# A two-level Strassen MLP: another order of the pair's steps, two splits of w2 in other buffers, two sums of x two steps later

## The chip, the cores and the metric

The kernel runs on one core of one Trainium2 chip. The metric is the device time of one execution in microseconds (us), the median of the runs. A core has five engines with instruction queues of their own: TensorE (PE, matmuls), VectorE (DVE), ScalarE (ACT), GpSimd (POOL) and SyncE (SP, which here only issues DMAs). An engine takes its instructions in the order in which the program gives them, and waits at one until its operands and its buffer are free.

## The reference

```python
h = x @ w1                                             # x (8, 1024, 1024), w1 (1024, 4096)
h = 0.5 * h * (1 + tanh(sqrt(2 / pi) * (h + 0.044715 * h ** 3)))
return h @ w2                                          # w2 (4096, 1024)
```

Input and output are float32. The kernel multiplies 16-bit floats and sums in float32.

## The kernel before

The 8192 rows of x are worked off in eight superblocks of 1024 tokens (0 to 7). For each, the first multiplication makes h = x·w1, ScalarE applies the gelu and leaves g in SBUF in 16 bits, and the second multiplication makes g·w2. Both use Strassen's scheme, seven products of halves in place of eight: an operand of a product is a quarter block of the matrix (11, 12, 21, 22) or a sum of such blocks, made on DVE or POOL in 16 bits, and the result needs float32 additions of what the products left in PSUM. Superblocks 0 and 1 use one level. From superblock 2 on ("late") a second level is used inside products 1 to 7, in both multiplications. What the second level of w1 and w2 needs (inner sums) is made once, in superblocks 0 and 1, and stored in DRAM; that of x has to be made for each superblock.

**The late first multiplication** (`matmul1_late`, L780-822). The columns of h are worked off in eight pairs of chunks, j = 0 to 7, and a ninth round, j = 8, finishes the last one. What a pair does is the list `PAIR` (L30-36), 108 steps, walked once for each j. A step that has a ' behind its name belongs to the pair before. So the list is a software pipeline written out, and each engine's order is the order of its steps in the list (the instructions are pinned in program order). The first letter names the kind:

- `m` and `h` are PE's: `m36` is inner product 6 of product 3 (two matmuls of 256 columns into a quarter of a PSUM bank), `h40` half of product 4, which has one level (four matmuls of 512 columns). In pair 0 products 1, 5 and 7 are whole too: they have no inner sums to wait for.
- `z`, `e`, `s`, `u` are float32 sums on DVE that read PSUM (L138); `a`, `c`, `p`, `q` and `z11`, `z51`, `z71` are copies on ScalarE (L165); `g` is a gelu on ScalarE (L510).
- `v` is a float32 sum on POOL (L764), `d` a difference of two blocks of g (L516; on POOL, for pair 0 on DVE).
- `x35` is inner sum 5 of the x operand of product 3, made on DVE; `X35` is the same on POOL (both L355, `inner_sum`). They are made once in a superblock: those without a mark while j = 0, those with a ' while j = 1. The sums of product 7 lie in a tile "xi", the others in tiles "gc". Sum 6 reads sum 7 or 5, and sum 4 or 3 reads sum 6, of the same product.
- `k` is one of four sums of w1 for the next pair, on POOL (L315, tiles "mu"), from pair 2 on. `b` and `r` are sums of blocks of g that the second multiplication begins with, on POOL (L1059).

At j = 8 the table `BEGIN` starts the first quarters of the second multiplication behind the named steps. At the end of each round j = 0 to 3 `x_cast_paced` (L475-480) brings a quarter of the next superblock's x into DRAM in 16 bits: POOL copies two elements of a chunk of g as a mark, which makes it wait for that chunk, and then issues two casting DMAs (L472). For j > 3 SP's transposing DMAs read them. The weights of a pair (`StoredHalf`, loads at L284) are loaded by SP up to three pairs ahead into tiles of the pool `up`.

**The late second multiplication** (`matmul2`, class `Inner`): seven products of seven steps each in the order 4, 1, 2, 5, 6, 7, 3. The table `FILL_2` names the jobs that DVE does behind step n of product m, as "mn: jobs". `n6` and `n3` are sums 6 and 3 of the next superblock's x blocks (two of the operands of its first multiplication); they stand at 33 and 34, steps 3 and 4 of the last product.

**Superblock 1's second multiplication** (`matmul2_made`) has one level. Beside it, the table `FILL` (second half of the kernel's two tables, one for superblock 0 and one for 1) makes the inner sums of w2, "splits": `p34` is inner sum 4 of w2's operand of product 3 (`split_jobs`, L968-982). One split is two DVE sums of 128x1024 into a tile of 4 KB for each partition, and a DMA issued by POOL (L980) that stores it.

**Buffers.** The pool `up` has 24 tiles of 4 KB named "u", for nearly everything that passes; `mp` two of the same size named "mu", for the made sums of w1; `gcp` four "gc"; `xip` one "xi"; `tp` nine float32 tiles "tmp"; PSUM has eight banks. A tile is handed out in turn, and its first writer waits until the last user of the buffer is done, be it an engine or a storing DMA.

The marking copy and the split's allocation are these lines:

```python
done = g["22"][:, 2 * j - 1, :] if j else now.temps["a", 0]          # L813, matmul1_late
nxt["xb"] = x_cast_paced(sb + 1, done, 2 * j, nxt.get("xb"), True)
t[n] = unit(NI // 2, OH // 2)                                        # L977, split_jobs: a "u" tile
```

Of the kernel before, what the change touches and what calls it, by code (L numbers as in the profile page):

```python
# [9 lines left out]
DT = mybir.dt.float16  # L10
# [4 lines left out]
P = 128  # L15
# [12 lines left out]
MADE_HALF = 3  # L28
ROOM = (("11", 4), ("11", 8), ("11", 12), ("22", 4), ("22", 8), ("22", 12), ("21", 4), ("21", 8), ("21", 12))
PAIR = """  # L30
X37' s1' g220' m11 g110' m15 u1' m36' m27' c1 e30' r1' X35 x55 m51 z11 z32' h41' m16 k7 z23'
m32' m33' z24' z51 g221' x54' v0' k6 x15 m56 m55 z12 x36 m37' q1' g120' e31' x75 m71 X34' c5 m52
z71 m24' m13 g111' z52 m12 m17 z33' m76 m75 z34' z13 m53 m57 v1' m21 m25 b a0 x17 h60 m34' z53
c7 r0 p0 m14 x77 k5 g210' z72 k3 e20 m77 s0 g211' m54 z73 m73 X74' z21 m72 x57 a1 X56 h40 x16
g121' m26 d' u0 z22 m31 p1 z31 x76 q0 e21 r2' h61 m74 m23 m22 m35 X14
""".split()
BEGIN = {"m32": (0,), "m33": (1,), "m24": (2, 3), "m34": (4,)}
SPLIT_IN_M1 = ()


def slots(table):
# [24 lines left out]
    ;51:g311 g312;52:g321 g322;53:a67;54:a66;55:a65;56:a63  # L66
    ;61:n5;63:a77;64:a76;65:a75;66:a73;67:n7
    ;71:y11 y12;72:y21 y22;73:a37;74:a36 w11;75:a35 w12;76:a33 w21;77:w22
    ;31:z11 z12;32:z21 z22;33:n6;34:n3""".replace("\n    ", ""))


@with_exitstack
def kernel(
# [18 lines left out]
    NI = I // P // 2  # L92
    OH = O // 2
# [10 lines left out]
    mp = ctx.enter_context(tc.tile_pool(name="mp", bufs=2))  # L104
# [29 lines left out]
    def unit(rows, cols):  # L134
        return up.tile([P, rows, cols], DT, name="u")

    def tt(out, in0, in1, op, pin=False):
        i = nc.vector.tensor_tensor(out=out, in0=in0, in1=in1, op=op)  # L138
        if pin:
            tc.keep_in_program_order(i)  # L140
# [12 lines left out]
    def chunks(t):  # L153
        return t.rearrange("p o (c n) -> p o c n", c=QC)
# [203 lines left out]
    def x_blocks():  # L358
        return {b: unit(KH, HT) for b in ("22", "21", "12", "11")}
# [107 lines left out]
    def x_cast(s, after, rows=range(0, SB, P), xb=None):  # L467
        if xb is None:
            xb = xdram.tile([SB, H], DT, name="xb")
        with tc.issue_after(after.ins):  # L470
            for q in rows:
                nc.gpsimd.dma_start(out=xb[q:q + P, :], in_=x2[s * SB + q:s * SB + q + P, :])  # L472
        return xb

    def x_cast_paced(s, g_chunk, q, xb, pin=False):  # L475

        mark = nc.gpsimd.tensor_copy(out=pace, in_=g_chunk[:, :2])
        if pin:
            tc.keep_in_program_order(mark)
        return x_cast(s, mark, range(q * P, (q + 2) * P, P), xb)  # L480

    def x_transpose(xb, dma, blocks=None, which=range(4)):
        blocks = blocks or x_blocks()
        for b, t in [list(blocks.items())[i] for i in which]:
            a, k = int(b[0]) - 1, int(b[1]) - 1
            for j in range(KH):
                dma(
                    t[:, j, :],
                    xb[a * HT:(a + 1) * HT, (k * KH + j) * P:(k * KH + j + 1) * P],
                    transpose=True,  # L490
                )
        return blocks
# [30 lines left out]
    def g_tiles():  # L523
        return {b: g_tile(b) for b in ("11", "12", "21", "22")}
# [249 lines left out]
    def matmul1_late(xs, sb, quads, g):  # L774
        n = NI // 2
        nxt = {}
        early = Inner(4, g["22"])
        made = set(xs.inner)
        last = None
        for j in range(n + 1):  # L780
            if j < n:
                quads += [StoredHalf(i) for i in range(len(quads), min(j + 3, n))]
                now = Pair(j, quads[j], xs, g)
            for key in PAIR:
                late = key.count("'")
                key = key.rstrip("'")
                if key[0] in "xX":
                    if late == j and int(key[1]) not in made:
                        xs.inner_sum(int(key[1]), int(key[2]), nc.vector if key[0] == "x" else nc.gpsimd)
                elif key == "b":  # L790
                    if 4 <= j < n:
                        early.make_quarter(7, j - 4)
                elif key[0] == "r":
                    if j == n - 1 + late:
                        early.make_quarter(6, int(key[1]))
                elif key[0] == "k":
                    if MADE_HALF <= j + 1 < n:
                        quads[j + 1].make(int(key[1]))
                elif late:
                    for i in BEGIN.get(key, ()) if j == n else ():  # L800
                        early.begin(i)
                    if last is not None:
                        last.run(key)
                elif j < n:
                    now.run(key)
            last = now
            if j == n:
                break
            if j == n - 1:
                early.load(STEPS[:3])  # L810
            if sb < NSB - 1:
                if j < 4:
                    done = g["22"][:, 2 * j - 1, :] if j else now.temps["a", 0]  # L813
                    nxt["xb"] = x_cast_paced(sb + 1, done, 2 * j, nxt.get("xb"), True)
                if j == 3:
                    nxt["blocks"] = x_blocks()
                if j > 3:
                    x_transpose(nxt["xb"], load_in_order, nxt["blocks"], range(j - 4, j - 3))
        blocks = nxt.get("blocks")
        return g, early, None if blocks is None else XOps(blocks)  # L820
# [145 lines left out]
    def split_jobs(m, pieces):  # L966
        t = {}

        def operand(v, h):
            if isinstance(v, int):  # L970
                return t[v][:, h * QC:(h + 1) * QC, :]
            k, b = int(v[0]) - 1, int(v[1]) - 1
            return chunks(pieces()[2 * k + h])[:, b]

        def make(n):
            u, op, v = W_SUM[n]
            t[n] = unit(NI // 2, OH // 2)  # L977
            for h in range(2):
                tt(t[n][:, h * QC:(h + 1) * QC, :], operand(u, h), operand(v, h), op, True)
            nc.gpsimd.dma_start(out=in_d[m][:, SUMS.index(n)], in_=t[n])  # L980

        return [lambda n=n: make(n) for n in SUMS]
# [242 lines left out]
    for sb in range(NSB):  # L1225
        if sb < 2:
            g, nxt = matmul1(xs, sb, quads, first if sb == 0 else None)
            xs, quads = matmul2_made(sb, g, None if sb else quads[-1].keep_raw, nxt)
            continue
        g, early, nxt = matmul1_late(xs, sb, quads, g_late or g_tiles())  # L1230
        g_late, quads = matmul2(sb, g, early, nxt)
        xs = nxt
# [30 lines left out]
```

## Time and profile before

| | |
|---|---|
| median of 3 runs | 1485.46 us (1484.85 to 1492.23) |
| profiled execution | 1482.05 us |
| its span, first to last instruction | 1480.3 us |
| mean granted clock of TensorE | 0.996 |
| busy: PE / DVE / ACT / POOL | 1455.5 / 1223.9 / 690.4 / 622.0 us |
| matmuls | 10635 |
| moved by DMA | 472.72 MB, mean 319 GB/s |

The profile is a trace of one execution. PE, DVE, ACT and POOL are the engines above; SPq is the queue of SyncE, DMA issues only. A group or an instruction is named by its line in the kernel, its engine and operation, and out<-in by the program's tile names; "[2.86 <-DVE ps L138]" says that the engine had been idle for 2.86 us and that an instruction of DVE, of line 138, ended that wait. The list of waits sums these up by engine: total us, times, longest. The chain of waits follows the work that ended last back from the end of the span and is shown in order of time: start, us, who held it. A line of windows gives for a stretch of time its length, the busy time of PE, PE's weight load (PEld), DVE, ACT and POOL with the number of their instructions, PE's granted clock as a share of full speed, the share of the DMA engines' time in use, and GB/s.

### The profile page before, as it was taken

The page shows a single profiled execution, that of the slowest core. Times are in us where ns is not written, and L with a number is a line of the kernel's source. Part 1 is how long each engine was busy: PE and PEld are TensorE (multiplying, and loading weights), DVE is VectorE, ACT ScalarE, POOL GpSimd, SP SyncE. Part 2 cuts the span into 40 slices and gives each one's busy share as a digit, 9 for nine tenths or more (in the row PEclk, how much of TensorE's full clock was granted, in tenths as well). Part 3 has the DMA queues.
Part 4 walks back from the last instruction along what each step waited for, and adds up shares of the span by engine and source line. Part 5 has one row for each costly group of instructions (what it writes and reads, how often), then busy time and mean ns, then how long its engine had stood idle before and what let it go on. Part 6 is the DMA issues. An engine that isn't in the chain of part 4 may idle for free.

```text
span 1480.3 us, 28812 instructions
## 1 busy us (share of the span) xinstructions
PE 1455.5 (98%) x10635; PEld 1038.9 (70%) x10635; DVE 1223.9 (83%) x2031; ACT 690.4 (47%) x1406; POOL 622.0 (42%) x632
## 2 busy tenths in 40 slices
PE   8999999999999999999999999999999999999998
PEld 5444444444467887678877788677886778877887
DVE  5656668657788999889998899888998889988897
ACT  5665116631078511784128831388213872168610
POOL 1541232212369312782047811487104971158411
PEclk9999999999999999999999999999999999999999
DMA  9999999879999999999999999999999999997897
GB/s 328 345 346 382 280 362 343 293 253 264 346 325 232 328 335 381 361 234 367 312 377 347 227 376 316 360 320 239 375 334 358 292 282 343 368 383 233 294 299 233
DMA packets 205709, 472.72 MB, mean 319 GB/s; under 512 B 75648, under 2 KB 80768, under 8 KB 204672
## 3 DMA queue, kind: packets, MB, share of 16 engines
q1 hardware_dynamic: 177632, 373.35, 73.4%
q0 software_dynamic: 27936, 97.53, 22.0%
q8 instruction: 83, 1.36, 0.4%
q14 instruction: 58, 0.48, 0.1%
HBM read 370.15 MB, written 115.34 MB: 328 GB/s over the span
## 4 chain that ended last, share of the span: by engine, by line
PE 68%; DVE 3%; issue 1%; DVEq 0%
PE ps L1082 35%; PE ps L712 22%; PE ps L497 11%; DVE tmp L138 1%; DVE gc L355 1%; DVE ps L138 1%; DVE xi L355 0%; DVE u L138 0%; DVEq L138 0%
## 5 line engine op out<-in xcount | busy, mean ns | idle before, releaser
L165 ACT COPY tmp<-ps 128x512 f32<-128x512 f32 (+1 forms) x536 | 280.6, 536 | 294.9 <-PE ps L1124 139.2
L497 PE MATMUL ps<-u 128*128 128x512 f16 x1552 | 363.9, 379 | 0.0
L1082 PE MATMUL ps<-u,gc 128*128 128x256 f16 x2688 | 300.3, 273 | 0.0
L1082 PEld LDWEIGHTS <-gc 128*128 128x128 f16 x2688 | 263.0, 98 | 30.5
L138 DVE TENSOR_TENSOR tmp<-tmp,ps 128x256 f32<-128x256 f32 (+1 forms) x372 | 198.4, 544 | 79.4 <-PE ps L1124 29.5
L497 PEld LDWEIGHTS <-u 128*128 128x128 f16 x1552 | 152.1, 98 | 146.8 <-issue 0.5
L138 DVE TENSOR_TENSOR u<-u 128x1024 f16<-128x1024 f16 (+3 forms) x292 | 221.2, 800 | 36.2 <-DMA w_d<-u 20.9
L839 POOL DMA_DIRECT2D out_dram<-u x70 | 63.8, 952 | 442.3 <-DVE u L138 239.5
L1082 PE MATMUL ps<-u,g 128*128 128x256 f16 x2016 | 231.8, 273 | 0.0
L712 PEld LDWEIGHTS <-u 128*128 128x128 f16 x2026 | 197.7, 98 | 48.1 <-issue 0.8
L165 ACT COPY u<-ps 128x512 f32<-128x512 f32 (+1 forms) x134 | 78.0, 587 | 327.9 <-PE ps L1082 320.9
L1082 PEld LDWEIGHTS <-g 128*128 128x128 f16 x2016 | 197.3, 98 | 24.1
L712 PE MATMUL ps<-u 128*128 128x256 f16 x1342 | 204.9, 273 | 0.3 <-DVE tmp L138 0.2
L138 DVE TENSOR_TENSOR ps<-tmp,ps 128x256 f32<-128x256 f32 x444 | 177.3, 424 | 25.5 <-PE ps L712 16.0
L510 ACT ACTIVATE g<-tmp 128x512 f16<-128x512 f32 x282 | 173.4, 634 | 47.0 <-DVE tmp L138 46.7
L1124 PE MATMUL ps<-u,g 128*128 128x512 f16 x768 | 168.3, 382 | 2.8 <-DVE tmp L138 2.8
L138 DVE TENSOR_TENSOR u<-u,ps 128x512 f32<-128x512 f32 x216 | 146.4, 682 | 26.4 <-PE ps L1082 17.7
L510 ACT ACTIVATE g<-ps 128x512 f16<-128x512 f32 x230 | 137.7, 599 | 51.8 <-PE ps L712 42.8
L1124 PEld LDWEIGHTS <-g 128*128 128x128 f16 x768 | 75.5, 98 | 94.9 <-issue 5.3
L764 POOL TENSOR_TENSOR tmp<-tmp 128x512 f32<-128x512 f32 x96 | 121.8, 1269 | 41.8 <-ACT tmp L165 37.8
L138 DVE TENSOR_TENSOR tmp<-ps,tmp 128x512 f32<-128x512 f32 x126 | 87.0, 690 | 55.9 <-PE ps L497 45.9
L138 DVE TENSOR_TENSOR gc<-g,gc 128x2048 f16<-128x2048 f16 x78 | 95.0, 1218 | 0.6
(68 smaller groups left out, 1470.4 us busy)
## 6 DMA issues: line engine op xcount, KB each, us to landing
u<-w_d SPq DMA_DIRECT2D x353, 512.0 KB, 8.8
u<-in_d SPq DMA_DIRECT2D x168, 512.0 KB, 9.3
out_dram<-u POOLq DMA_DIRECT2D x70, 512.0 KB, 10.2
gc<-in_w_dram SPq DMA_DIRECT2D x48, 512.0 KB, 5.9
g<-w_d SPq DMA_DIRECT2D x45, 512.0 KB, 14.6
w_d<-u POOLq DMA_DIRECT2D x40, 512.0 KB, 7.7
w_d<-u SPq DMA_DIRECT2D x32, 512.0 KB, 7.9
in_d<-u POOLq DMA_DIRECT2D x28, 512.0 KB, 6.3
```

Source lines behind the costliest of these rows:

```text
L138: i = nc.vector.tensor_tensor(out=out, in0=in0, in1=in1, op=op)
L165: tc.keep_in_program_order(nc.scalar.copy(out=out, in_=in_))
L355: engine.tensor_tensor(out=operand(j), in0=operand(u), in1=operand(v), op=op)
L497: tc.keep_in_program_order(nc.tensor.matmul(bank, lhsT=w, rhs=x, start=first and k == 0, stop=k == n - 1, skip_group_check=not first,))
L510: gelu_last[0] = nc.scalar.activation(out=out, in_=src, func=GELU, scale=scale)
L712: tc.keep_in_program_order(nc.tensor.matmul(out, lhsT=w, rhs=x, start=first and k == 0, stop=k == 1, skip_group_check=not first,))
L764: tc.keep_in_program_order(nc.gpsimd.tensor_tensor(out=t, in0=t, in1=temp("p", m), op=ADD))
L839: return nc.gpsimd.dma_start(out=rows, in_=src, **kw)
L1082: tc.keep_in_program_order(nc.tensor.matmul(bank[:, i * OH // 2:(i + 1) * OH // 2], lhsT=t[:, c, i * P:(i + 1) * P], rhs=self.y[j][:, c, : ...
L1124: tc.keep_in_program_order(nc.tensor.matmul(pair(bank), lhsT=a[:, c, :], rhs=chunks(pieces[c // QC])[:, :, c % QC, :], start=(first and c ...
```

## The change

Four edits, with no change of what is computed.

1. `PAIR` gets another order of its 108 steps. Six sums of x change engine: `X37'`, `X35`, `X56` go from POOL to DVE (`x37`, `x35`, `x56`), `x54'`, `x57`, `x76` from DVE to POOL (`X54'`, `X57'`, `X76'`). After it, all ten sums that DVE makes stand in round 0, and of POOL's six `X57'`, `X76'`, `X34'`, `X74'`, `X54'` stand in round 1 and `X14` in round 0. The steps `z22`, `z31`, `m22`, `m23`, `m26`, `m35` move into the next round (they get a '), and `g220'` moves into its own. `BEGIN` starts the first five quarters of the second multiplication behind other steps.
2. `FILL_2`: `n6` moves from step 33 to 34 and `n3` from 34 to 36.
3. The mark ahead of the casts of x is the own pair's chunk 2j of block 22 of g (step `g220`), in place of chunk 2j − 1 (for j = 0 in place of the temporary a0).
4. Splits 7 and 4 of w2 take a "mu" tile, where they took a "u" tile.

In the changed kernel one line is gone at L813, so the lines behind it have numbers smaller by one (L1082 is L1081, L980 is L979).

```diff
 PAIR = """
-X37' s1' g220' m11 g110' m15 u1' m36' m27' c1 e30' r1' X35 x55 m51 z11 z32' h41' m16 k7 z23'
-m32' m33' z24' z51 g221' x54' v0' k6 x15 m56 m55 z12 x36 m37' q1' g120' e31' x75 m71 X34' c5 m52
-z71 m24' m13 g111' z52 m12 m17 z33' m76 m75 z34' z13 m53 m57 v1' m21 m25 b a0 x17 h60 m34' z53
-c7 r0 p0 m14 x77 k5 g210' z72 k3 e20 m77 s0 g211' m54 z73 m73 X74' z21 m72 x57 a1 X56 h40 x16
-g121' m26 d' u0 z22 m31 p1 z31 x76 q0 e21 r2' h61 m74 m23 m22 m35 X14
+m26' h41' z31' q1' r1' x77 v0' m11 s1' m15 x35 x36 z22' u1' X57' c1 m36' m35' m32' X76' m51 e30'
+m55 z11 m27' z32' g221' z51 m23' c5 x15 k7 m22' z23' v1' m16 g110' m37' z24' x75 X34' z12 b r0
+m33' m52 m56 g120' e31' m24' k6 g111' m71 m75 z71 x17 m13 m12 z52 m17 m53 z33' c7 k5 X74' m21
+m57 m72 a0 z34' X54' m76 m25 z13 z53 h60 x55 m34' p0 g210' m14 x56 r2' k3 x16 z72 m77 X14 g211'
+h40 m54 g121' e20 s0 z73 x37 z21 a1 d' e21 m73 m31 h61 q0 u0 m74 p1 g220
 """.split()
-BEGIN = {"m32": (0,), "m33": (1,), "m24": (2, 3), "m34": (4,)}
+BEGIN = {"m37": (0,), "m24": (1,2), "m34": (3, 4)}
...
-    ;31:z11 z12;32:z21 z22;33:n6;34:n3""".replace("\n    ", ""))
+    ;31:z11 z12;32:z21 z22;34:n6;36:n3""".replace("\n    ", ""))
...
                 if j < 4:
-                    done = g["22"][:, 2 * j - 1, :] if j else now.temps["a", 0]
-                    nxt["xb"] = x_cast_paced(sb + 1, done, 2 * j, nxt.get("xb"), True)
+                    nxt["xb"] = x_cast_paced(sb + 1, g["22"][:, 2 * j, :], 2 * j, nxt.get("xb"), True)
...
             u, op, v = W_SUM[n]
-            t[n] = unit(NI // 2, OH // 2)
+            t[n] = (mp.tile([P, NI // 2, OH // 2], DT, name="mu") if n in (7, 4) else unit(NI // 2, OH // 2))
```

## What is predicted

> **What bounds the kernel now.** I read the page first, then TensorE's waits, the chain that ended last, and the timeline around the waits that the chain names.
>
> ```profile
> PE 1455.5 (98%) x10635; PEld 1038.9 (70%) x10635; DVE 1223.9 (83%) x2031; ACT 690.4 (47%) x1406; POOL 622.0 (42%) x632
> ```
>
> ```profile
> PE ps L712 <- DVE ps L138: 13.3, 9, 2.9
> PE ps L1124 <- DVE tmp L138: 2.8, 1, 2.8
> ```
>
> ```profile
> 499.32 83.40 PE ps L1082 x764
> 582.72 2.59 PE ps L497 x12
> ...
> 594.88 1.31 DVE gc L355
> ...
> 599.21 2.13 PE ps L712 x18
> ...
> 607.64 0.86 PE ps L497 x4
> 608.50 3.93 PE ps L712 x36
> ...
> 619.60 3.93 PE ps L712 x36
> ...
> 677.78 83.40 PE ps L1082 x764
> ...
> 1217.00 83.40 PE ps L1082 x764
> ...
> 1392.44 83.42 PE ps L1082 x764
> ```
>
> TensorE (PE) is busy 98% of the span, and its matmul count is the bound: the second multiplication runs without a gap (83.40 us for 764, 0.109 each). In the late first multiplication one pair of column chunks takes 619.60 − 608.50 = 11.10 us. Its 70 matmuls of 256 columns (3.93 / 36 = 0.109 each) and 16 of 512 (0.86 / 4 = 0.215) need 11.1, so a pair in its stride loses nothing. A late superblock repeats every 677.78 − 499.32 = 178.5 us, and the last one in 1392.44 − 1217.00 = 175.4. What can be won is PE's waits: 13.3 us in nine waits for VectorE (DVE) and 2.8 in one. The chain shows where: about 16 us after a late multiplication begins (582.72) it leaves PE for a DVE sum of x (L355), and the same stretch returns at superblocks 4, 5 and 6.
>
> The timeline there, then the same step in the last superblock, where no wait follows (columns: start, us, instruction, in brackets the idle time before it):
>
> ```profile
> 593.83 1.28 POOL L764 TENSOR_TENSOR tmp<-tmp 128x512 f32<-128x512 f32 x1
> ...
> 594.88 3.94 DVE L355 TENSOR_TENSOR gc<-u,gc 128x512 f16<-128x512 f16 x1
> 595.06 1.16 POOL L355 TENSOR_TENSOR gc<-u,gc 128x512 f16<-128x512 f16 x1
> ...
> 596.17 1.26 POOL L764 TENSOR_TENSOR tmp<-tmp 128x512 f32<-128x512 f32 x1
> 597.39 1.14 POOL L355 TENSOR_TENSOR xi<-u,xi 128x512 f16<-128x512 f16 x1
> ...
> 598.75 0.41 DVE L138 TENSOR_TENSOR ps<-tmp,ps 128x256 f32<-128x256 f32 x1
> ...
> 599.21 0.38 PE L712 MATMUL ps<-u,mu 128*128 128x256 f16 x2 [2.86 <-DVE ps L138]
> ```
>
> ```profile
> 1311.55 1.16 POOL L355 TENSOR_TENSOR gc<-u,gc 128x512 f16<-128x512 f16 x1
> ...
> 1312.56 0.43 DVE L355 TENSOR_TENSOR gc<-u,gc 128x512 f16<-128x512 f16 x1
> 1312.82 1.29 POOL L764 TENSOR_TENSOR tmp<-tmp 128x512 f32<-128x512 f32 x1
> ```
>
> One 16-bit sum takes 0.43 us where GpSimd (POOL) has a pause and 3.94 where four POOL sums follow each other without one. It ends when POOL's row of sums ends (598.5), and the f32 additions behind it on DVE release the bank that PE wants. A smaller form of it stands earlier in each entry:
>
> ```profile
> 585.76 1.36 DVE L355 TENSOR_TENSOR gc<-u,gc 128x512 f16<-128x512 f16 x1 [1.58 <-POOL gc L355]
> ```
>
> The Trainium skill, page "SBUF — State Buffer", section "SBUF: two separate sides", calls the port pair of these two engines an exclusive lock that the first comer holds for its whole instruction. By that alone the sum waits for one POOL sum; the rows show four, so the measurement decides.
>
> **The change, part by part.** (a) *The order.* PE's matmuls are the same. Six of the sums of x change engine, three each way: DVE makes its ten all in pair 0, and POOL five of its six in pair 1, where DVE has no 16-bit work left but one difference of g. So the four long waits (4 × 2.86) and the short ones should go: 13.3 us, the full row; I bound it below by 11.4. In pair 0 nine DVE sums now stand in a row (9 × about 0.4 = 3.5 us) just after the entry, beside POOL's stores of out. Row for two such sums and a store at once:
>
> ```profile
> 583.43 0.75 DVE L355 TENSOR_TENSOR gc<-u 128x512 f16<-128x512 f16 x2
> 583.82 0.72 POOL L839 DMA_DIRECT2D out_dram<-u  x1 [0.50 <-PE ps L497]
> ```
>
> Neither is drawn out. [...] PE needs none of these sums before pair 1: products 1, 5 and 7 of pair 0 are whole, and of product 3 pair 0 runs only the quarter that takes x as it is. Pair 0's 36 matmuls of 512 columns and 6 of 256 take 36 × 0.215 + 6 × 0.109 = 8.4 us, more than twice 3.5. The f32 additions queued behind the sums on DVE wait for those same products. Cost taken: 0; if that cover were gone, 3.5 us at each of six entries is the other end, and 0 is nearest to the row.
>
> What is late next? First, POOL's sums of w1 for the following pair, which begin in pair 2 and use a load behind the casts of x:
>
> ```profile
> 600.92 10.30 SPq L284 DMA_DIRECT2D u<-w_d  x7
> ...
> 608.44 1.15 POOL L315 TENSOR_TENSOR mu<-u 128x512 f16<-128x512 f16 x1 [8.63 <-DVE ps L138]
> ```
>
> POOL idled 8.6 us before it and began as the load landed (about 608.3). With no 2.9 us wait, pair 2 begins at about 602.2 (582.72 + 8.4 + 11.1), and POOL, which has a casting pair (1.01) and one f32 sum (1.28) ahead of it, gets there some 3 us later, at about 605.2: 3.1 us before the old landing. Against that the change moves the casts: their mark waits for the pair's own last gelu (L813) rather than an older one, so pair 1's casts, now at
>
> ```profile
> 598.81 1.01 POOL L472 DMA_DIRECT2D xb<-in_x_dram  x2
> ```
>
> go out when pair 1 ends, about 602.5, and leave the DMA engines free ahead of that load, which SP issues from 600.92 on. The cost is between 0 (the load lands that much earlier) and 3.1 us per entry, at four entries (superblocks 3 to 6). I take 0.5 each, 2.0 in all, since the sums lead their use by most of a pair.
>
> (b) *The two x sums, two steps later* (n6, n3), each four of the 0.43 us quarters, 1.7 at most. The DVE additions of the seventh step wait for PE anyway, and DVE ends with PE there; 0, and 1.7 for each of the five entries if that cover is gone.
>
> (c) *Splits 7 and 4 in the small pool's buffers.* The early wait of 2.8:
>
> ```profile
> 191.36 3.57 SPq L162 DMA_DIRECT2D w_d<-u  x4
> 194.68 2.43 DVE L138 TENSOR_TENSOR u<-u 128x1024 f16<-128x1024 f16 x3 [8.63 <-DMA w_d<-u]
> 195.04 18.07 SPq L198 DMA_DIRECT2D u<-w_d  x8
> ...
> 197.76 15.66 PE L1124 MATMUL ps<-u,g 128*128 128x512 f16 x64 [2.79 <-DVE tmp L138]
> ...
> 208.69 7.70 DVE L138 TENSOR_TENSOR u<-u 128x2048 f16<-128x2048 f16 x14 [1.83 <-DMA u<-w_d]
> ```
>
> The split of product 3 by sum 4 wants a u buffer whose store SyncE (SP) issues only at 191.36, as the first of four; DVE stands 8.63 us, and the addition that frees PE's bank is behind it. In the small pool the buffer's last user is the split by sum 4 of product 2, four splits earlier, stored by POOL itself and not by SP, so the wait of 2.79 goes. But the loads at 195.04 keep their time, and DVE already waits 1.83 for one at 208.69; with all work earlier that wait grows. Give-back between 0 and 2.8; 0.8 taken.
>
> (d) *Clock.* The windows around three of these waits, granted clock in the third column from the end, then DMA share and GB/s:
>
> ```profile
> 190.00:198.00 8.00, 5.21 (x26) 2.25 (x24) 3.32 (x5) 0.00 (x0) 0.53 (x1) 1.00 0.98 324
> 198.00:206.00 8.00, 8.00 (x31) 3.31 (x30) 6.67 (x8) 0.59 (x1) 2.71 (x5) 0.79 1.00 354
> ...
> 956.00:964.00 8.00, 7.29 (x44) 5.00 (x44) 6.20 (x16) 4.60 (x9) 1.31 (x4) 0.79 1.01 342
> ...
> 1137.00:1145.00 8.00, 8.00 (x49) 5.29 (x47) 6.12 (x16) 5.27 (x10) 0.36 (x1) 0.79 1.02 355
> ```
>
> After three of the five long waits the clock is 0.79 for 8 us: (1 − 0.79) × 8 = 1.68 us each, 5.0 in all, gone with the waits.
>
> **Sum.** 13.3 + 2.8 + 5.0 = 21.1 removed; 2.0 + 0.8 = 2.8 given back; 18.3 gained. The profiled execution took 1482.05, 1.77 over its span of 1480.3; that makes 1463.8. The median of the runs, 1485.46, is 3.4 above it, so I forecast **1467**.
>
> **The rivals.** *The load becomes the bound* at superblocks 3 to 6: half of the 3.1 us is lost, 1.6 × 4 = 6.4 in place of 2.0: 1472. For it: POOL already waits for that load. Against: the later casts. *The dips stay*: the clock falls for another cause, and 5.0 is not won: 1472. For it: two equal waits (superblocks 3 and 4) were followed by none. The Trainium skill, page "TensorE: Matmul & The Clock Gate", section "HAM oscillation — how this bites in real kernels", asks for idle gaps over about 3.4 us before the clock falls; no wait here is so long, and yet three were followed by a fall, so by that rule these dips had another cause, and by the rows they had these waits.
>
> *Transfers set the rate*: the DMA share is 0.98 to 1.02 in all windows above, and the waits come back at loads: about 1483, only 2.8 won. Against: at such shares the rate moved from 324 to 355 GB/s, so the share is not a ceiling of bytes.
>
> *Slower: the bank of product 5.* In the new order PE fills a bank with h41' and wants it again for m51 after five quarter products (5 × 2 × 0.109 = 1.09 us). ScalarE's copy q1' (0.59 by its group) must lie between, with handovers that I put at 0.25 together (DVE's end at 599.16 to PE at 599.21 is 0.05 of it):
>
> ```profile
> L165 ACT COPY tmp<-ps 128x512 f32<-128x512 f32 x410 | 238.3, 586 | 286.3 <-PE ps L1124 139.2 <-PE ps L497 116.2 <-PE ps L712 22.1
> L510 ACT ACTIVATE g<-ps 128x512 f16<-128x512 f32 x230 | 137.7, 599 | 51.8 <-PE ps L712 42.8 <-PE ps L430 4.4 <-PE ps L497 1.2
> ```
>
> The margin is 0.25 us in each of 7 pairs × 6 superblocks = 42. Right ahead of q1' in ScalarE's order stands the gelu g220, which waits for DVE's u0. If u0 is late by one f32 sum (0.41, the row at 598.75) when h41' ends, q1' comes 0.41 + 0.60 later and each pair loses 1.01 − 0.25 = 0.76, 32 in all: 1499. The gain is used up where 18.3 / 42 + 0.25 = 0.69 us stand ahead. Slower by over 0.5% it is from 0.86. For it: g220 follows u0, DVE is the busier of the two in a pair, and this is the tightest reuse in the list. Against: h41' itself, 4 matmuls of 512 columns (0.86), runs after p1, the copy ahead of g220, so g220 has as long to finish.
>
> **How the numbers follow.** Forecast 0.53 (its own range 1461 to 1470: nothing given back and a median as near its profile as 1482.05 − 21.1, to twice the 2.8 given back), load 0.17, dips 0.10, transfers 0.12, slower 0.08. The range 1461 to 1481 holds the first three (0.80) and their sum, 1467 + 4.4 + 5.0 = 1476.4, with the rest of the early give-back (2.0) and 1.7 at one or two entries. 0.5%, about what a measurement of this kernel can tell from no change, is 7.4 us: the first three are faster (0.80), transfers within (0.12), the bank slower (0.08).
>
> **What would show it.** Right: no wait of PE for DVE at L712 over 0.3 us, no 16-bit DVE sum over 1 us at L355, no L1124 wait, clock 1.00 throughout, late superblocks repeating every 175.4 us rather than 178.5. The load rival shows as waits of PE or idle POOL before L315 in pair 2; the dips as 0.79 windows without a wait; transfers as DVE or PE waiting for DMA; the bank as PE waiting for ScalarE (ACT) some 0.8 us in every pair. A period unchanged at 178.5 would prove me wrong on the collision.

## The result, and the profile after

The changed kernel takes 1461.13 us (median of 6 runs, 1458.54 to 1468.21) against 1485.98 us (6 runs, 1484.83 to 1492.23) for the kernel before: a ratio of 0.9831, 95% interval 0.9803 to 0.9860. The forecast was 1467, with a range of 1461 to 1481; the ratio applied to the 1485.46 from which the forecast was made gives 1460.4, just below that range. The kernel is faster by the mechanism that was named, and by 6 us more than the sum said.

The profiled execution took 1458.54, which is 23.5 less than that of before. Two lines of its page, then all of PE's waits:

```profile
span 1456.8 us, 28781 instructions
...
PE 1448.3 (99%) x10635; PEld 1037.5 (71%) x10635; DVE 1212.3 (83%) x2029; ACT 681.2 (47%) x1406; POOL 623.2 (43%) x634
```

```profile
PE ps L407 <- DVE tmp L399: 1.8, 4, 1.0
PE ps L365 <- DVE warm L1219: 1.2, 1, 1.2
PE ps L1081 <- DMA u<-in_d: 0.6, 1, 0.6
PE ps L430 <- ACT u L165: 0.5, 1, 0.5
PE ps L430 <- DVE u L226: 0.4, 1, 0.4
```

The nine waits at L712 and the one at L1124 (now L1123) are gone. What is left is the start of the kernel and one wait of 0.6 for a load that had not been late before. Look at PE's busy time too: for the same 10635 matmuls it is 7.2 us less than the 1455.5 of before. A list of waits alone does not tell of that part.

The chain of waits in order of time, the starts of the second multiplications:

```profile
844.57 83.40 PE ps L1081 x764
...
1019.51 83.40 PE ps L1081 x764
...
1194.45 83.40 PE ps L1081 x764
...
1369.40 83.42 PE ps L1081 x764
```

The late superblocks repeat every 174.94 us (1019.51 − 844.57; the next two are the same within 0.01), where 178.5 stood, and 175.4 for the last. The timeline of superblock 3's entry shows where the sums of x went:

```profile
578.69 0.42 DVE L355 TENSOR_TENSOR xi<-u 128x512 f16<-128x512 f16 x1
...
579.07 0.73 POOL L838 DMA_DIRECT2D out_dram<-u  x1 [1.58 <-DVE u L138]
...
582.18 1.15 POOL L355 TENSOR_TENSOR gc<-u,gc 128x512 f16<-128x512 f16 x1 [2.38 <-DVE gc L355]
582.88 0.73 DVE L355 TENSOR_TENSOR gc<-u 128x512 f16<-128x512 f16 x1
...
586.86 1.29 POOL L764 TENSOR_TENSOR tmp<-tmp 128x512 f32<-128x512 f32 x1
588.09 1.17 POOL L355 TENSOR_TENSOR gc<-u 128x512 f16<-128x512 f16 x1
...
593.76 1.15 POOL L355 TENSOR_TENSOR gc<-u,gc 128x512 f16<-128x512 f16 x1
```

DVE makes its sums from 578.69 on, POOL's store beside them takes 0.73 as before, and POOL's seven sums follow each other from 586.86 to 594.9 with no 16-bit sum of DVE among them. One pair still meets: x37 at 582.88 beside POOL's X14 takes 0.73 in place of 0.42, and PE does not wait for it. In the groups by shape, the form that took 1522 ns on average is down to 423 (first the kernel before, then the changed one):

```profile
L355 DVE TENSOR_TENSOR gc<-u,gc 128x512 f16<-128x512 f16 x17 | 25.9, 1522 | 8.5 <-POOL gc L355 8.5
L355 DVE TENSOR_TENSOR gc<-u,gc 128x512 f16<-128x512 f16 x17 | 6.7, 423 | 0.4
```

POOL's first sum of w1 in pair 2, which the prediction named as late next, and the casts ahead of it:

```profile
598.53 1.01 POOL L472 DMA_DIRECT2D xb<-in_x_dram  x2
599.55 1.28 POOL L764 TENSOR_TENSOR tmp<-tmp 128x512 f32<-128x512 f32 x1
601.40 1.16 POOL L315 TENSOR_TENSOR mu<-u 128x512 f16<-128x512 f16 x1 [0.56 <-DVE ps L138]
```

The row names DVE, but the trace's landing event of the load stands at 601.27, 0.13 ahead of the sum: it is still the load that releases it. It was issued at 586.50 and took 14.8 us, where it took 17.8 before (590.51 to 608.31). The prediction took it for one of the loads that SP issues from 600.92 on; by the landing it is one issued 10 us earlier, and the casts of two pairs, at 591.65 and 598.81, were issued while it was under way. The first product now begins at 577.81, so the load lands 23.5 us behind it, not 25.6, and POOL idles 0.56 instead of 8.6.

### The profile page after: what moved, and what is told of

The parts are those of the page before. It is cut to its first block, busy times and chain, and to the rows that moved or that the text cites. A ratio compares the mean times of both kernels' runs of the same rounds, so it can differ in the third digit from the quotient of the medians.

```text
span 1456.8 us, 28781 instructions
## 1 busy us (share of the span) xinstructions
PE 1448.3 (99%) x10635; PEld 1037.5 (71%) x10635; DVE 1212.3 (83%) x2029; ACT 681.2 (47%) x1406; POOL 623.2 (43%) x634
## 4 chain that ended last, share of the span: by engine, by line
PE 97%; DMA 3%; SPq 0%; DVE 0%; issue 0%; DVEq 0%
PE ps L1081 33%; PE ps L497 26%; PE ps L712 23%; PE ps L1123 13%; DMA u<-w_d 1%; DMA u<-in_d 1%; PE ps L430 1%; DMA gc<-in_w_dram 1%; SPq L162 0%; PE ps L407 0%; DVE u L226 0%; DVE u L138 0%; DVE u L418 0%; DVEq L138 0%; SPq L1033 0%
## 5 line engine op out<-in xcount | busy, mean ns | idle before, releaser
L165 ACT COPY tmp<-ps 128x512 f32<-128x512 f32 (+1 forms) x536 | 268.9, 540 | 311.5 <-PE ps L497 165.9
L1081 PE MATMUL ps<-u,gc 128*128 128x256 f16 x2688 | 300.3, 273 | 0.0
L1081 PEld LDWEIGHTS <-gc 128*128 128x128 f16 x2688 | 263.0, 98 | 30.4
L138 DVE TENSOR_TENSOR tmp<-tmp,ps 128x256 f32<-128x256 f32 (+1 forms) x372 | 199.7, 545 | 87.1 <-PE ps L712 29.5
L712 PEld LDWEIGHTS <-u 128*128 128x128 f16 x2026 | 198.3, 98 | 55.4
L1081 PE MATMUL ps<-u,g 128*128 128x256 f16 x2016 | 230.9, 273 | 0.6 <-DMA u<-in_d 0.6
L138 DVE TENSOR_TENSOR u<-u 128x2048 f16<-128x2048 f16 (+3 forms) x264 | 206.2, 820 | 27.6 <-DMA w_d<-u 9.9
L712 PE MATMUL ps<-u 128*128 128x256 f16 x1342 | 216.9, 273 | 0.0
L1081 PEld LDWEIGHTS <-g 128*128 128x128 f16 x2016 | 197.1, 98 | 23.8 <-DMA u<-in_d 1.0
L138 DVE TENSOR_TENSOR ps<-tmp,ps 128x256 f32<-128x256 f32 x444 | 181.3, 426 | 19.4 <-PE ps L712 12.2
L138 DVE TENSOR_TENSOR u<-u,ps 128x512 f32<-128x512 f32 x216 | 147.1, 683 | 26.8 <-PE ps L1081 17.5
L1123 PE MATMUL ps<-u,g 128*128 128x512 f16 x768 | 166.4, 379 | 0.0
L1123 PEld LDWEIGHTS <-g 128*128 128x128 f16 x768 | 75.1, 98 | 90.7
L138 DVE TENSOR_TENSOR tmp<-ps,tmp 128x512 f32<-128x512 f32 x126 | 86.8, 690 | 54.5 <-PE ps L497 42.5
L764 POOL TENSOR_TENSOR tmp<-tmp 128x512 f32<-128x512 f32 x96 | 122.0, 1273 | 20.1 <-DVE tmp L138 13.3
L712 PE MATMUL ps<-gc,mu 128*128 128x256 f16 x504 | 96.2, 273 | 0.0
```

The lines of the kernel that those rows point to most:

```text
L165: tc.keep_in_program_order(nc.scalar.copy(out=out, in_=in_))
L712: tc.keep_in_program_order(nc.tensor.matmul(out, lhsT=w, rhs=x, start=first and k == 0, stop=k == 1, skip_group_check=not first,))
L764: tc.keep_in_program_order(nc.gpsimd.tensor_tensor(out=t, in0=t, in1=temp("p", m), op=ADD))
L1081: tc.keep_in_program_order(nc.tensor.matmul(bank[:, i * OH // 2:(i + 1) * OH // 2], lhsT=t[:, c, i * P:(i + 1) * P], rhs=self.y[j][:, c, : ...
L1123: tc.keep_in_program_order(nc.tensor.matmul(pair(bank), lhsT=a[:, c, :], rhs=chunks(pieces[c // QC])[:, :, c % QC, :], start=(first and c ...
```

## The experiments

Each ratio compares a run with executions of the kernel before that were taken beside it; their medians were 1486.9 to 1489.9, and the ratio is not exactly the quotient of two medians.

**What ended the standstill.** The theory: a 16-bit sum of DVE stands still while POOL's sums follow each other, the additions queued behind it release PE's bank late, and the clock falls after some of these stops. The rivals: the sum waits for one POOL instruction only; or PE waits for the sum's result; or the splits made the gain.

First, one step of the changed kernel put back to DVE, in the middle of the new row of POOL sums:

```diff
-... z22' u1' X57' c1 m36' ...
+... z22' u1' x57' c1 m36' ...
```

> The changed kernel with one step put back to DVE in the round where POOL's sums stand in a row: x57' for X57'. If a DVE sum stands still until POOL's row of sums pauses, it lasts about 4 to 6 us (from about 588 to the end of the row, 593), PE waits 3 to 5 us at each of four to six entries, and clock dips follow some of them: 15 to 30 us slower than the changed kernel, about the time before. If it waits for one POOL instruction only, it lasts under 1.7 us, PE waits nowhere, and the time is that of the changed kernel within 2 us.

Measured: 1500.23 us, ratio to before 1.0083 (1.0050 to 1.0116), where the changed kernel has 0.981 to 0.983 in all its runs. Its timeline, then PE's waits:

```profile
595.67 6.47 DVE L355 TENSOR_TENSOR gc<-u 128x512 f16<-128x512 f16 x1
596.17 1.16 POOL L355 TENSOR_TENSOR xi<-u,xi 128x512 f16<-128x512 f16 x1
...
600.72 1.14 POOL L355 TENSOR_TENSOR gc<-u,gc 128x512 f16<-128x512 f16 x1
...
603.06 0.58 PE L712 MATMUL ps<-gc,g 128*128 128x256 f16 x2 [5.11 <-DVE ps L138]
```

```profile
PE ps L712 <- DVE ps L138: 24.8, 5, 5.1
```

One sum of 0.4 us lasts 6.47 and ends at 602.14, 0.28 behind POOL's row (601.86). At five of the six entries it stands still in this way (5.78 us at the first, 6.47 at the other four), and all five stops of PE come with a slower clock, some 9 us more by the pitch of the matmuls in the trace. The loss is larger than expected. The rival with one instruction is out. So is the one in which PE waits for the sum's result: the list names a float32 addition of L138 as what ended these waits, and in the kernel before the matmul that stood still (599.21) reads tiles u and mu, while the sum lies in gc.

Then the one sum alone, in the kernel before:

```diff
-... z51 g221' x54' v0' k6 ...
+... z51 g221' X54' v0' k6 ...
```

> The kernel before with one step changed: sum 4 of product 5 on POOL (X54') in place of DVE, at its old place in the list, in all late superblocks. Theory (only that sum's standstill made the long waits): the four waits of 2.9 and the dips of superblocks 5 and 6 go, the short ones of 0.25 and that of L1124 stay: 4 x 3.0 + 3.4 = 15.5 us, ratio 0.9896. If the dips had another cause: 12 us, ratio 0.992. Rival (PE waited for the result of the sum, or POOL's row of sums is itself too long, and is now 1.2 us longer): under 4 us.

Measured: 1481.46 us, ratio 0.9938 (0.9913 to 0.9964), by the ratio six tenths of the gain expected. The long waits at the entries are gone. Others came in their place, in pairs 2 and 3:

```profile
612.43 1.15 POOL L315 TENSOR_TENSOR mu<-u 128x512 f16<-128x512 f16 x1 [7.54 <-PE ps L712]
...
615.72 0.38 PE L712 MATMUL ps<-xi,u 128*128 128x256 f16 x2 [0.89 <-DVE ps L138]
...
618.83 0.38 PE L712 MATMUL ps<-u 128*128 128x256 f16 x2 [1.00 <-ACT g L510]
```

POOL's first sum of w1 again starts 0.13 behind its load's landing (612.30, 18.4 us after the issue), and PE waits twice for what follows. By the starts of the matmuls the trace loses 2.2 to 2.6 us so at each of superblocks 3 to 6, 9.6 in all. This is the prediction's rival of the load, at a higher price than its 1.6. The wait at L1124, 2.8 in the trace of before, is 5.7 here.

Next the other end of the collision: the sum stays on DVE at its place, and POOL's row is cut.

```diff
-... m71 X34' c5 ... z73 m73 X74' z21 ...
+... m71 x34' c5 ... z73 m73 x74' z21 ...
```

> The kernel before with X34' and X74' made on DVE instead, so that x54' stays on DVE at its place but POOL's row around it has a pause behind v0'. If a 16-bit DVE sum stands still as long as POOL's sums follow each other: x54' takes under 1.3 us in place of 3.94, no sum of x on DVE takes over 2.5, and the waits of 2.9 us at the entries shrink to under 1.3. If the length of the row does not matter: x54' still takes over 3 us and the waits stay. The time itself is confounded by the late loads of pairs 2 and 3 that the run with one sum moved showed: about 1475 to 1482.

One execution: 1484.16 us, above the expected 1475 to 1482. Around x54' (597.71):

```profile
596.66 2.70 POOL L764 TENSOR_TENSOR tmp<-tmp 128x512 f32<-128x512 f32 x2
597.71 0.52 DVE L355 TENSOR_TENSOR gc<-u,gc 128x512 f16<-128x512 f16 x1
598.90 0.74 DVE L355 TENSOR_TENSOR gc<-u,gc 128x512 f16<-128x512 f16 x1
```

It takes 0.52 beside two POOL sums, and the entries have only waits of 0.25. It came in where one POOL sum ended and the next began; the two together took 0.2 longer than two without a gap (1.22 from the start of one to the next, by the rows at 596.17 and 597.39 of before, and 1.28 for the last). Whether a gap let DVE in or DVE's turn made the gap, this trace does not tell. The time is lost again in pairs 2 and 3, and in a wait of 4.4 at L1124.

Last the whole list, with `BEGIN` and the later mark, without the splits and the moved sums of x (edits 1 and 3 of the change):

> The kernel before with the new list, BEGIN and the later mark of the casts; the splits and the two sums of x stay as before. Theory (16-bit sums of DVE stood still while POOL's sums followed each other): all nine waits of PE for DVE at L712 go, 13.3 us as listed and 0.16 more for each (a matmul of 256 columns takes 0.273 but the next follows after 0.109, so each stop costs the pipeline's filling too), and the two clock dips of superblocks 5 and 6, 3.4: about 18 us, ratio 0.988; the wait of 2.8 at L1124 and the dip behind it stay. Rival (the splits or the two moved sums made most of the gain): under 12 us, ratio over 0.992.

Measured: 1467.39 us, ratio 0.9852 (0.9821 to 0.9882), 4 us more than expected and inside the interval. Every wait at L712 is gone. The one at L1124 (here L1123) is there, and larger than in the trace of before; one at superblock 3's pair 2 is left. So the splits did not make most of the gain:

```profile
PE ps L1123 <- DVE tmp L138: 5.3, 1, 5.3
PE ps L497 <- ACT tmp L165: 2.3, 1, 2.3
PE ps L1081 <- DMA u<-in_d: 1.3, 1, 1.3
```

**The splits and the order of SP.** The kernel before with edit 4 alone:

```diff
-            t[n] = unit(NI // 2, OH // 2)
+            t[n] = (mp.tile([P, NI // 2, OH // 2], DT, name="mu") if n in (7, 4) else unit(NI // 2, OH // 2))
```

> The kernel before with splits 7 and 4 in the small pool's tiles alone. Theory: the wait of 2.8 at L1124, 0.2 of filling and the dip of 1.7 go and nothing is given back at the loads of superblock 1: about 4.7 us, ratio 0.9968. The prediction's give-back of 0.8: 3.9 us. Rival (the loads keep their time and PE waits there instead): 2 us or less.

Measured: 1483.42 us, ratio 0.9969 (0.9950 to 0.9987), or 4.6 us: the theory's size. No wait at L1124, and none for the loads of superblock 1. But waits for stored splits appear late in superblocks 2 to 5, and those at the entries stay:

```profile
PE ps L712 <- DVE ps L138: 12.7, 9, 2.9
PE ps L1082 <- DMA u<-in_d: 5.4, 4, 2.1
```

The size of the early wait is a matter of SP. (It stands in superblock 0's second multiplication, at `p34` of the first `FILL` table; `matmul2_made` serves both superblocks.) SP issues sixteen transposes of x there, behind them four stores of w2's block 22, the first of which holds the split's buffer, and behind these the loads of superblock 1's w1. How long the transposes take differs between executions of one kernel, here between 24.6 and 37.6 us. Two traces of the changed kernel, the first of them the one shown above:

```profile
167.53 24.60 SPq L162 DMA_TRANSPOSE u<-xb  x16
192.18 3.85 SPq L162 DMA_DIRECT2D w_d<-u  x4
```

```profile
167.53 37.59 SPq L162 DMA_TRANSPOSE u<-xb  x16
...
205.17 3.72 SPq L162 DMA_DIRECT2D w_d<-u  x4
...
217.39 8.89 PE L497 MATMUL ps<-u 128*128 128x512 f16 x27 [8.77 <-DMA u<-w_d]
```

All traces with SP's order of before, by the time at which the stores begin:

| stores begin, us | splits in | PE waits, us |
|---|---|---|
| 191.36 (the kernel before) | u | 2.8 at L1124 |
| 193.86, 194.22, 194.40, 194.81 | u | 5.3, 4.4, 5.7, 5.3 there |
| 189.39 to 193.16 (four, the changed kernel's first trace among them) | mu | 0 |
| 194.56, 196.42, 196.75 | mu | 1.1, 1.1, 1.8 for superblock 1's loads |
| 199.70, 204.24, 205.17 | mu | 4.3, 8.3, 8.8 for these loads |

It is not only their length. In the four traces of the second row the transposes took nearly what they took before (23.75 to 24.58 us against 23.66), but SP began them 1.8 to 2.8 us later. The kernels of that row differ from the one before only in the late superblocks.

To see whether SP's order is the cause, the stores go ahead of the transposes in the kernel before, and nothing else:

```diff
+                    keep("22")
                     xs = XOps(x_transpose(xb, load_in_order))
-                    keep("22")
```

> The kernel before with SP's four stores of w2's block 22 issued ahead of the sixteen transposes of superblock 1's x instead of behind them; the splits keep their u tiles. If the wait at L1124 (2.8 in one trace, 4.4 to 5.7 in four others) is set by how long the transposes hold up the store whose buffer the split takes: it goes, without the small pool's tiles, with its clock dip: 4.6 to 7.5 us, ratio 0.995 to 0.997. If the split waits for that store's own time: it stays.

Measured: 1482.94 us, ratio 0.9964 (0.9942 to 0.9986), without a wait at L1124, though the transposes lasted until 200.1. So the wait was for the store behind the transposes, and either edit takes it away. The same exchange in the changed kernel, and the changed kernel beside it:

> The changed kernel with the same exchange on SP. The loads of superblock 1's w1 stand behind both, stores and transposes, so if SP's time for the two together sets when they are issued, nothing is won: within 2 us of the changed kernel. If the stores cost less while the queue is empty, the loads leave up to 3.9 us earlier and the waits of PE for them (0 to 3.1 us in the changed kernel's traces) shrink: 1 to 3 us faster.

> The changed kernel beside the two runs of this call, as their measure: ratio 0.983, PE waits of 0 to 3.1 us for the loads of superblock 1.

Measured: 1469.32 us, ratio 0.9852 (0.9829 to 0.9875), against 1462.95 us, 0.9811 (0.9790 to 0.9832). Nothing is won, and by the medians 6 us are lost, though the intervals just overlap; the loads still stand behind the transposes, which took 39.6 us in this trace, and PE waits 4.7 for them. No version tried here beats the changed kernel.

**The mark of the casts.** The kernel before with the one sum moved and a late mark, on the copy q0 of the own pair:

```diff
-                    done = g["22"][:, 2 * j - 1, :] if j else now.temps["a", 0]
-                    nxt["xb"] = x_cast_paced(sb + 1, done, 2 * j, nxt.get("xb"), True)
+                    nxt["xb"] = x_cast_paced(sb + 1, now.temps["q", 0], 2 * j, nxt.get("xb"), True)
```

> The kernel before with sum 4 of product 5 on POOL, as in the run of one sum alone, and the mark of the casts on the copy q0 of the own pair, late in the round. If early casts in front of the load made that run's waits of PE in pairs 2 and 3 (9.6 us in all), they go: ratio 0.986 to 0.988, against 0.9938 without the mark. If the loads are late whatever the mark is: 0.994.

Measured: 1472.80 us, ratio 0.9908 (0.9875 to 0.9941), between the two. In its trace the load takes 16.6 us, and the waits of pairs 2 and 3 are 2.8 us in all by the starts of the matmuls, where the same kernel with the old mark lost 9.6. Then the changed kernel with the old mark, twice, each time beside the changed kernel:

```diff
+                    done = g["22"][:, 2 * j - 1, :] if j else now.temps["a", 0]
-                    nxt["xb"] = x_cast_paced(sb + 1, g["22"][:, 2 * j, :], 2 * j, nxt.get("xb"), True)
+                    nxt["xb"] = x_cast_paced(sb + 1, done, 2 * j, nxt.get("xb"), True)
```

> The changed kernel with the old mark, so that the casts of x go out earlier in each pair. If the load of w1 for POOL's sums in pair 2 becomes the bound once the collision is gone, and the later mark is what prevents it (the run that moved one sum alone lost 2.2 to 2.6 us there at each of superblocks 3 to 6): such waits of PE return in pairs 2 and 3, 7 to 10 us in all, ratio 0.988 to 0.990. If the mark does not matter: within 2 us of the changed kernel.

> The changed kernel once more, on the chip of the runs beside it, as their measure: ratio 0.983, no waits of PE for DVE, clock 1.00.

> The changed kernel with the old mark of the casts once more, beside the changed kernel on the same chip, since its first interval (0.984 to 0.991) touches that of the changed kernel. If the later mark carries a part of the gain: 4 to 8 us slower than the changed kernel. If not: within 2.

> The changed kernel beside the other runs of this call: ratio 0.983, a few waits for loads, no wait at L712, clock 1.00.

Measured: 0.9875 (0.9840 to 0.9910) against the changed kernel's 0.9823 (0.9799 to 0.9847), and the second time 0.9866 (0.9835 to 0.9898) against 0.9828 (0.9796 to 0.9861). By the ratios that is 8 and 6 us slower, but the intervals overlap. PE's waits in the second trace with the old mark:

```profile
PE ps L497 <- ACT tmp L165: 4.3, 4, 1.6
PE ps L497 <- DMA u<-w_d: 4.3, 1, 4.3
```

The first line is the load's chain in pair 2 of superblocks 3 to 6 (18.5 us from issue to landing); the changed kernel beside it has 1.1 in one such wait. The second line is the early loads, which have nothing to do with the mark. Of the 7 to 10 us of waits that were expected, the two traces with the old mark show 1.8 and 4.3. So about 3 us of the mark's worth are seen in the traces; that it carries more is not shown.

**The two sums of x.** The changed kernel with `33:n6;34:n3`, as before:

> The changed kernel with the two sums of x at steps 33 and 34, as before. The prediction's reading (DVE has room in either place): within 1 us of the changed kernel. Rival (the earlier sums hold DVE's additions or wait for the transposed x, which now comes late against PE): 0.5 to 1.7 us at each of five entries, 3 to 8 us slower.

Measured: 1465.34 us, ratio 0.9850 (0.9810 to 0.9890) against 0.9823, and 1460.91 in the traced execution against 1461.93 of the changed kernel's. No difference can be told.

**Transfers.** The changed kernel without the casts of superblocks 4 to 7:

> The changed kernel without the casting DMAs for superblocks 4 to 7 (their x is taken from superblock 3's copy, so their output is that of other tokens); the marks stay. Tells what transfers still cost in the changed kernel: if the few waits for loads of w1 and of the splits, 0.6 to 2.3 us in its two profiles, come from the DMA engines' load, those of superblocks 4 to 7 go and up to 2 us are won, ratio 0.981 to 0.983. If transfers still set the pace of the late superblocks, more: under 0.980.

Measured: 1461.82 us, ratio 0.9812 (0.9774 to 0.9850) against 0.9828 for the changed kernel beside it: no difference can be told. From superblock 2 on its trace has one wait for a load, 0.5 us; the four traces of the changed kernel have 0.4 to 3.4.

## Why the prediction was right and wrong

- *The collision* was right in place and price: the long waits go when the sum is moved and when POOL's row is cut, and one sum put back into a row costs 24.8 us of waits. That the new order might not do what it says is out.
- *The clock* was right as a sum: it is 1.00, and the 5.0 us went with the waits. The rival that *the dips stay* is out. Apart from the last microseconds of the span, the 17 traces have 23 stretches at half clock, and each stands at a stop of PE of 2.3 us or more. By the pitch of the matmuls in all traces, 18 stops with listed waits of 2.3 to 2.9 us were followed by a slower clock 10 times, 13 of 4.3 and more every time, shorter ones never. The windows around the four equal waits of 2.9 in the kernel with edit 4 alone, of which two were followed by a slower clock:

```profile
595.00:603.00 8.00, 7.63 (x46) 5.20 (x46) 6.39 (x16) 5.13 (x10) 0.98 (x3) 0.80 1.02 354
777.00:785.00 8.00, 7.47 (x57) 5.56 (x57) 7.57 (x20) 5.49 (x11) 1.13 (x3) 1.00 1.02 352
957.00:965.00 8.00, 7.56 (x46) 5.15 (x46) 6.52 (x18) 5.19 (x10) 1.04 (x3) 0.81 1.02 356
1139.00:1147.00 8.00, 8.00 (x62) 6.02 (x62) 7.22 (x18) 5.93 (x12) 0.58 (x2) 1.00 1.02 357
```

  The Trainium skill, page "TensorE: Matmul & The Clock Gate", section "What's actually happening", has the clock decided in windows of 3413 ns that run on by themselves. The traces agree: in that of before the granted clock falls to half at 198.83, 956.59 and 1137.50 us, for 3.41 us each time, and the starts lie 757.76 and 180.91 us apart, 222 and 53 times 3.413; in the other traces the halved stretches last 3.41, 6.83 or 10.24 us.

  That answers why equal waits ended unequally. Cut each trace into windows of 3.413 us that begin where its clock falls, and take for each of the 35 stops of over 1.5 us the largest share of one window in which PE stood idle. The 23 stops with 0.59 or more had the clock halved, the 12 with 0.58 or less had not. A stop of 2.86 us that a window's end divides falls short (0.54 at 599.21, no dip); one that lies almost within a window does not (0.80 at 956.71, a dip). So the size of 5.0 rested on where the stops of this one execution fell.
- *The sum* is the step that failed, at "13.3 + 2.8 + 5.0 = 21.1 removed; 2.0 + 0.8 = 2.8 given back". The first part lacked a term. A matmul of 256 columns takes 0.273 us by its group and the next one follows after 0.109, so a stop costs 0.273 − 0.109 = 0.164 more than the list of waits says, which counts from the end of the last matmul; the filling hides in PE's busy time. With 11 stops in the trace of before (nine at L712 for one releaser, one for another, one at L1124) that is 1.8 us. The ledger of the two traces: PE's listed waits fell from 20.1 to 4.5 in all, so 15.6; PE's busy time by 7.2, of which the clock is 5.0 and the filling 1.8; together 22.8 of the span's 23.5. The low end of the range, 1461, stood for nothing given back but left out the filling too, and so the result came out under it.
- The second part was too much for this execution. After the early part of the kernel 0.6 was given back, for one stored split, and nothing at the loads of w1, not 2.0. The load rival was real, 2.4 us a superblock in the kernel with one sum moved, but with the later mark the load takes 14.8 to 17.0 us there in the four traces of the changed kernel, against 16.7 to 19.3 in the two with the old mark. Superblock 1's loads gave back nothing, not 0.8, and in other executions up to 8.8; the 2.8 of the early wait is 4.4 to 5.7 in four traces of kernels that are the same up to there. Here the prediction took one execution for the kernel: the one in which PE waits 8.8 for those loads took 1473.03, and a forecast of 1467 could have been met by such waits through luck alone. Of the 5.9 us between forecast and median, the filling makes 1.8, the give-back 2.2 (2.8 less 0.6), and the distance of the median from its profile 0.8 (2.6 in place of 3.4); 1.1 is not accounted for.
- *The moved sums of x* at nothing: no difference can be told. *Transfers set the rate*: not as a rate, though single loads are late. *The bank of product 5*: no wait of PE for ACT in the first trace of the changed kernel beyond the start; no experiment of its own was made.

Open is why sixteen transposes take 24.6 us in one execution and 37.6 in another of the same kernel. Between the fastest and the slowest trace of the changed kernel (1458.54 and 1473.03) the wait behind them makes 8.8 of the 14.5 us.

## What to carry to other kernels

Where two engines hold each other up, look for a short instruction of one beside an unbroken row of the other: it can stand still for the whole row, and what is queued behind it pays. Price a stop of PE at its listed wait, the refilling of the pipeline and the chance of a slower clock (here, that it leaves PE idle for 0.59 of one window of 3.41 us), and expect the load that it covered to be late next: move what competes with that load in the same edit. Before a wait behind a DMA queue goes into a sum, look at a second execution.

## What was not expected of the hardware

A DVE sum of 0.4 us lasted 6.47 us beside six POOL sums in a row, float32 and 16-bit ones alike, not one turn of about 1.2. SP's same sixteen transposes took 24.6, 26.5, 28.6 and 37.6 us in four executions of one kernel. A stop of PE of 2.86 us, well short of a window of 3.41, was enough for a window at half clock when it left PE idle for 0.59 or more of one window.
